# The start of the stationary weights in their ring buffers, one value for all segments against one for each

## The chip, the cores and the metric

The kernel runs on one core of a Trainium2 chip. The metric is the device time of one execution in microseconds. A core has engines that run side by side: TensorE (PE: matmuls, and PEld: the loads of their stationary operand), VectorE (DVE), ScalarE (ACT), GpSimd (POOL) and SyncE (SP), which here issues nearly all DMAs. TensorE reads both operands of a matmul from the on-chip memory SBUF: a 128x128 stationary part, which is loaded first, and then the moving columns, which stream past it into PSUM.

## The reference

One layer of a hybrid model over 256 tokens of width 1024: a modulated RMS norm of x, one projection `h @ w_in` to 11272 columns, a causal attention of eight heads with a relative bias (the query block has no earlier block here), a chunkwise mLSTM of four heads, two output projections, two sigmoid gates, and a last projection, added to x.

```
h = rmsnorm(x, norm_w) * (1 + scale) + shift          # shift, scale, gate from c @ w_ada + b_ada
qa, ka, va, za, qm, km, vm, zm, om, ig, fg, ga, gm = split(h @ w_in)
ya = (attention(rmsnorm(qa), rmsnorm(ka), va, rel_bias) * silu(za)) @ w_att_proj
qm, km = split(silu(causal_conv([qm, km])))
hm = rmsnorm(sigmoid(om) * mlstm(qm, km, vm, ig, fg))
ym = (hm * silu(zm)) @ w_ml_proj
out = x + gate * ((sigmoid(ga) * ya + sigmoid(gm) * ym) @ w_out)
```

## The kernel before

Each product of a projection is made of three passes in a reduced fp32 format (fp32r): an operand `a` is split into a high part (`a` rounded to fp32r) and a low part (`a` minus the high part), and the passes are high by high, high by low and low by high. A first phase makes `h`, transposed, as `hTh` and `hTl` (8 blocks of 128 features, 256 tokens each), and with it the columns of q and most of k. What follows is a list of 25 chunks of up to 512 columns, two to a segment (`va`, `za`, `qm`, and so on, in the order of the `seg` calls; the first chunk, of `ka`, stands alone). The loop that the program walks is over groups: one group is two of a chunk's eight blocks of 128 features, so there are four groups to a chunk.

Two kinds of chunk are told apart. In a `tok` chunk the stationary operand is a 128x128 part of `hTh` or `hTl` (`yh` or `yl` in the last segment) and the weights move, 512 columns at a time (lines 935 to 937, and 954 to 956 in the last chunk). In a `ws` chunk the weights are stationary: a group holds 24 matmuls (two feature blocks, four parts of 128 columns, three passes, lines 942, 944 and 945), and each loads a new 128x128 part of the weights and moves 256 columns of `hTh` or `hTl` past it. In `att` the moving tiles are `yah` and `yal`, in `ml` `ymh` and `yml`. The segments of the `ws` kind are `za`, `qm`, `km`, `att`, `ga`, `gm` and `ml`: 14 chunks, 1344 matmuls.

The weights of a group come by DMA into a tile `raw`, issued some groups ahead; `split` (line 416) then makes `wh` on ScalarE (line 423) and `wl` on VectorE (line 427; on GpSimd in eight groups) four groups ahead of the matmuls. `wh` and `wl` have five buffers each (`HB`), used in turn, so that group g uses buffer g mod 5. A buffer has 1152 floats to a partition (`RING`), 1024 of which are used: in a `tok` chunk from the buffer's start, in a `ws` chunk from float 80, which is byte 320 (`WS_AT`, line 25, used at lines 420 to 422).

Between groups the program puts other work of TensorE by hooks tied to the group's number: transposes against the identity (`ident`, lines 467, 604 to 606, 775), the attention's and the mLSTM's own products (lines 579, 617, 718, 738). The first matmul of a group after such work is called a restart here. The order of all work is written out by hand.

Of the kernel before, what the change touches and what calls it, by code (L numbers as in the profile page):

```python
# [21 lines left out]
NEG = -1e30  # L22
BUCKETS = 32

RING, WS_AT = 1152, 80

COL = dict(qa=0, ka=1024, va=2048, za=3072, qm=4096, km=5120, vm=6144, zm=7168, om=8192,
           ig=9216, fg=9220, ga=9224, gm=10248)
# [36 lines left out]
def tile_hybrid(ctx: ExitStack, tc: tile.TileContext, x, c, params, params2, rel_t, w_row, ada_mod, ada_gate,  # L65
# [232 lines left out]
    chunks = []  # L298
# [117 lines left out]
    def split(g, between=()):  # L416
        li, ks, cs = raw_of[g]
        w = rawt[li][:, ks, cs]
        n = chunks[g // 4]["n"]
        at0 = WS_AT if chunks[g // 4]["kind"] == "ws" else 0  # L420
        h = hl.tile([128, RING], F32R, name="wh", bufs=HB)[:, at0:at0 + 1024].rearrange("p (k n) -> p k n", k=2)[:, :, 0:n]
        l = hl.tile([128, RING], F32R, name="wl", bufs=HB)[:, at0:at0 + 1024].rearrange("p (k n) -> p k n", k=2)[:, :, 0:n]
        nc.scalar.copy(h, w)  # L423
        for fn, a in between:
            fn(*a)
        e = nc.gpsimd if g in pool_lo else nc.vector
        e.tensor_tensor(l, w, h.bitcast(F32), op=OP.subtract)  # L427
        whl[g] = (h, l)
# [462 lines left out]
    for g in range(A):  # L891
        split(g)
        for fn, a in early.get(g, []):
            fn(*a)
        consumed.update(li for li in cons.get(g, []) if li not in gate_loads)
    pump()
    for g in range(NG):
        ci, kp = divmod(g, 4)
        ch = chunks[ci]
        if g + A < NG:  # L900
            split(g + A, hooks_between.get(g, []))
            consumed.update(li for li in cons.get(g + A, []) if li not in gate_loads)
# [101 lines left out]
```

## Time and profile before

| | us |
|---|---|
| three timed executions | 355.11, 355.51, 355.52 |
| their median | 355.51 |
| the profiled execution | 354.88 |
| its span, first to last instruction | 353.1 |

The profiled execution's own time is 1.8 us more than its span. An engine's busy time is a sum over the span; matmuls are pipelined, so that the durations of two neighbours overlap. What a matmul costs in a stream is therefore not its duration but its pitch: the time from its start to the next one's start. The two go together for the `ws` matmuls, as the rows below show.

### The profile page before, as it was taken

What the parts mean: (1) busy time and instruction counts of PE and PEld (TensorE: products, weight loads), DVE (VectorE), ACT (ScalarE), POOL (GpSimd) and SP (SyncE); (2) the same over time, 40 slices, a digit from 0 to 9 for tenths busy, and PEclk for the clock granted to TensorE, in tenths of its full rate; (3) what the DMA queues carried; (4) which work ended last, traced back from release to release, by engine and by line L of the source; (5) the groups of instructions that cost most, each with busy time, mean ns of one, the idle gap of its engine ahead of it and who ended that gap; (6) DMA issues with size and microseconds to landing.
All of it is one profiled execution on the core that took longest, in us unless ns stands there. A gap on an engine that the chain in (4) does not pass through costs nothing.

```text
span 353.1 us, 5961 instructions
## 1 busy us (share of the span) xinstructions
PE 348.1 (99%) x2346; PEld 318.9 (90%) x2346; DVE 238.4 (68%) x362; ACT 212.7 (60%) x329; POOL 77.7 (22%) x89
## 2 busy tenths in 40 slices
PE   8999999999999999999999999999999999999995
PEld 5888889888999999999999888888899999999885
DVE  4799988879855528767774474764475775447773
ACT  3777799898786876674654435545646374534320
POOL 4920006583005043555240000000010320000000
PEclk9999999999999999999999999999999999999999
DMA  8999999994780463493664956749219129290011
GB/s 309 417 419 420 413 375 348 212 283 194 245 291 5 127 232 124 141 384 129 238 239 132 380 204 213 265 150 381 64 28 373 78 74 376 89 358 1 2 59 59
DMA packets 24573, 77.95 MB, mean 221 GB/s; under 512 B 2909, under 2 KB 5985, under 8 KB 24034
## 3 DMA queue, kind: packets, MB, share of 16 engines
q1 hardware_dynamic: 24240, 77.03, 61.2%
q10 hardware_dynamic: 306, 0.55, 0.5%
q8 instruction: 18, 0.29, 0.3%
q14 instruction: 9, 0.07, 0.1%
HBM read 76.12 MB, written 1.45 MB: 220 GB/s over the span
## 4 chain that ended last, share of the span: by engine, by line
PE 99%; DVE 0%; POOL 0%; issue 0%; POOLq 0%
PE mm L944 15%; PE mm L942 15%; PE mm L945 14%; PE mm L937 10%; PE mm L935 10%; PE mm L936 10%; PE pm L186 9%; PE pg L186 2%; PE xps L243 1%; PE pc L224 1%; PE mm L956 1%; PE mm L954 1%; PE aux L617 1%; PE warm L217 1%; PE mm L955 1%; PE aux L467 1%
## 5 line engine op out<-in xcount | busy, mean ns | idle before, releaser
L427 DVE TENSOR_TENSOR wl<-raw,wh 128x1024 fp32r<-128x1024 f32 (+1 forms) x92 | 112.5, 1234 | 66.9 <-ACT wh L423 66.9
L423 ACT CAST wh<-raw 128x1024 fp32r<-128x1024 f32 (+1 forms) x100 | 101.9, 1031 | 58.1 <-PE mm L937 29.7
L942 PE MATMUL mm<-hTh,wh 128*128 128x256 f32 x320 | 90.1, 282 | 0.0
L945 PE MATMUL mm<-hTh,wl 128*128 128x256 f32 x320 | 88.8, 278 | 0.0
L944 PE MATMUL mm<-hTl,wh 128*128 128x256 f32 x320 | 88.8, 278 | 0.0
L942 PEld LDWEIGHTS mm<-hTh,wh 128*128 128x128 f32 x320 | 60.4, 189 | 0.0
L944 PEld LDWEIGHTS mm<-hTl,wh 128*128 128x128 f32 x320 | 60.2, 188 | 0.0
L945 PEld LDWEIGHTS mm<-hTh,wl 128*128 128x128 f32 x320 | 60.1, 188 | 0.0
L935 PE MATMUL mm<-wh,hTh 128*128 128x512 f32 (+1 forms) x144 | 55.0, 382 | 0.0
L937 PE MATMUL mm<-wh,hTl 128*128 128x512 f32 (+1 forms) x144 | 54.4, 378 | 0.0
L936 PE MATMUL mm<-wl,hTh 128*128 128x512 f32 (+1 forms) x144 | 54.3, 377 | 0.0
L937 PEld LDWEIGHTS mm<-wh,hTl 128*128 128x128 f32 x144 | 27.0, 188 | 5.0
L936 PEld LDWEIGHTS mm<-wl,hTh 128*128 128x128 f32 x144 | 27.1, 188 | 4.7
L935 PEld LDWEIGHTS mm<-wh,hTh 128*128 128x128 f32 x144 | 27.0, 188 | 4.7
L427 POOL TENSOR_TENSOR wl<-raw,wh 128x1024 fp32r<-128x1024 f32 x8 | 19.6, 2463 | 17.9 <-ACT wh L423 12.6
L757 POOL TENSOR_SCALAR f<-f 128x4 f32<-128x4 f32 x2 | 0.4, 199 | 86.8 <-DVE f L756 86.8
L175 DVE TENSOR_TENSOR wrl<-raw,wrh 128x512 fp32r<-128x512 f32 (+1 forms) x24 | 18.0, 775 | 2.0 <-ACT wrh L170 1.7
L942 PE MATMUL mm<-yah,wh 128*128 128x256 f32 x64 | 18.0, 281 | 0.0
L944 PE MATMUL mm<-yal,wh 128*128 128x256 f32 x64 | 17.7, 277 | 0.0
L945 PE MATMUL mm<-yah,wl 128*128 128x256 f32 x64 | 17.7, 277 | 0.0
L942 PE MATMUL mm<-ymh,wh 128*128 128x256 f32 x64 | 17.7, 276 | 0.0
L944 PE MATMUL mm<-yml,wh 128*128 128x256 f32 x64 | 17.7, 276 | 0.0
(210 smaller groups left out, 648.9 us busy)
## 6 DMA issues: line engine op xcount, KB each, us to landing
raw<-in_w_in_dram SPq DMA_DIRECT2D x36, 1024.0 KB, 5.1
adat<-in_ada_mod_dram SPq DMA_DIRECT2D x16, 512.0 KB, 9.4
raw<-in_ada_gate_dram SPq DMA_DIRECT2D x4, 1024.0 KB, 5.7
raw<-in_w_att_proj_dram SPq DMA_DIRECT2D x4, 1024.0 KB, 7.5
raw<-in_w_ml_proj_dram SPq DMA_DIRECT2D x4, 1024.0 KB, 8.2
raw<-in_w_out_dram SPq DMA_DIRECT2D x4, 1024.0 KB, 5.6
raw<-in_w_row_dram SPq DMA_DIRECT2D x4, 896.0 KB, 12.3
raw<-in_w_row_dram SPq DMA_DIRECT2D x4, 640.0 KB
```

The costliest lines, as they stand in the source:

```text
L175: e.tensor_tensor(l[:, cs], wrow[k][:, cs], h[:, cs].bitcast(F32), op=OP.subtract)
L186: nc.tensor.matmul(pm[ch][:, t], a[:, k, t * 128:(t + 1) * 128], b[:, cs], start=k == 0 and i == 0 and (ch < 3 or t == 0), stop=k == KT - ...
L217: nc.tensor.matmul(pw[:, 0, 0:128], ident, ident, start=True, stop=True)
L224: nc.tensor.matmul(pc[n][:, 0:512], ones[0:1, :], crow[:, n * 512:(n + 1) * 512], start=True, stop=True)
L423: nc.scalar.copy(h, w)
L427: e.tensor_tensor(l, w, h.bitcast(F32), op=OP.subtract)
L935: nc.tensor.matmul(o, a, wh[:, kk], start=first, stop=False)
L936: nc.tensor.matmul(o, a, wl[:, kk], start=False, stop=False)
L937: nc.tensor.matmul(o, b, wh[:, kk], start=False, stop=last)
L942: nc.tensor.matmul(o, wh[:, kk, cs], sh_[:, k], start=first and i % 2 == 0, stop=False, skip_group_check=True)
L944: nc.tensor.matmul(o, wh[:, kk, cs], sl_[:, k], start=False, stop=False, skip_group_check=True)
L945: nc.tensor.matmul(o, wl[:, kk, cs], sh_[:, k], start=False, stop=last and i % 2 == 1, skip_group_check=True)
```

## The change

The one start of 80 floats for all `ws` chunks becomes a start by the segment's name: 84 floats (336 bytes) in `za` and `ml`, 80 (320) in `qm` and `km` as before, 76 (304) in `att`, 72 (288) in `ga` and 88 (352) in `gm`. The `tok` chunks have no entry and begin at the buffer's start, as before. The buffers keep their size and their places. No instruction is added, removed or moved on any engine and no wait differs: what differs is the address in the weight operand of 960 of the 1344 `ws` matmuls (five segments of 192), and in what the 80 instructions that fill those buffers write and, for `wl`, read.

```
-RING, WS_AT = 1152, 80
+RING = 1152
+WS_AT = dict(za=84, qm=80, km=80, att=76, ga=72, gm=88, ml=84)
...
         n = chunks[g // 4]["n"]
-        at0 = WS_AT if chunks[g // 4]["kind"] == "ws" else 0
+        at0 = WS_AT.get(chunks[g // 4]["name"], 0)
         h = hl.tile([128, RING], F32R, name="wh", bufs=HB)[:, at0:at0 + 1024].rearrange("p (k n) -> p k n", k=2)[:, :, 0:n]
         l = hl.tile([128, RING], F32R, name="wl", bufs=HB)[:, at0:at0 + 1024].rearrange("p (k n) -> p k n", k=2)[:, :, 0:n]
```

## Rows read from the trace of the kernel before

**Rows 1.** The page: busy time by engine, and the granted clock in 40 slices.

```profile
PE 348.1 (99%) x2346; PEld 318.9 (90%) x2346; DVE 238.4 (68%) x362; ACT 212.7 (60%) x329; POOL 77.7 (22%) x89
...
PEclk9999999999999999999999999999999999999999
```

**Rows 2.** Waits of PE over the span: line, releaser, total us, times, longest us.

```profile
PE warm L217 <- POOL ident masks.py:199: 1.4, 1, 1.4
```

**Rows 3.** The page: costliest groups, the splits of the weights and who they wait for.

```profile
L427 DVE TENSOR_TENSOR wl<-raw,wh 128x1024 fp32r<-128x1024 f32 (+1 forms) x92 | 112.5, 1234 | 66.9 <-ACT wh L423 66.9
L423 ACT CAST wh<-raw 128x1024 fp32r<-128x1024 f32 (+1 forms) x100 | 101.9, 1031 | 58.1 <-PE mm L937 29.7
```

**Rows 4.** Timeline of PE in `qm` and `km`: start us, duration us, line, operation.

```profile
130.01 0.28 PE L942 MATMUL mm<-hTh,wh 128*128 128x256 f32 x1
...
140.89 0.28 PE L942 MATMUL mm<-hTh,wh 128*128 128x256 f32 x1
```

**Rows 5.** Timeline of PE, fourth group of `za`: restart, and last three matmuls.

```profile
97.49 0.36 PE L942 MATMUL mm<-hTh,wh 128*128 128x256 f32 x1
97.69 0.28 PE L944 MATMUL mm<-hTl,wh 128*128 128x256 f32 x1
97.81 0.28 PE L945 MATMUL mm<-hTh,wl 128*128 128x256 f32 x1
...
100.28 0.28 PE L945 MATMUL mm<-hTh,wl 128*128 128x256 f32 x1
```

**Rows 6.** Groups by line, `za`'s first chunk: count, busy us, mean ns, idle before.

```profile
L945 PE MATMUL mm<-hTh,wl 128*128 128x256 f32 x32 | 9.0, 281 | 0.0
```

**Rows 7.** Groups by line, `za`'s second chunk.

```profile
L945 PE MATMUL mm<-hTh,wl 128*128 128x256 f32 x32 | 8.9, 278 | 0.0
```

**Rows 8.** Groups by line, `att`, both chunks.

```profile
L945 PE MATMUL mm<-yah,wl 128*128 128x256 f32 x64 | 17.7, 277 | 0.0
```

**Rows 9.** Groups by line, `ga`'s first chunk.

```profile
L945 PE MATMUL mm<-hTh,wl 128*128 128x256 f32 x32 | 8.9, 279 | 0.0
```

**Rows 10.** Groups by line, `ga`'s second chunk.

```profile
L945 PE MATMUL mm<-hTh,wl 128*128 128x256 f32 x32 | 9.0, 280 | 0.0
```

**Rows 11.** Groups by line, `gm`, both chunks.

```profile
L945 PE MATMUL mm<-hTh,wl 128*128 128x256 f32 x64 | 17.7, 276 | 0.0
```

**Rows 12.** Groups by line, `ml`, both chunks.

```profile
L945 PE MATMUL mm<-ymh,wl 128*128 128x256 f32 x64 | 17.7, 276 | 0.0
```

**Rows 13.** Timeline of PE, `tok` matmuls in the middle of the span.

```profile
192.19 0.39 PE L936 MATMUL mm<-wl,hTh 128*128 128x512 f32 x1
...
214.86 0.39 PE L937 MATMUL mm<-wh,hTl 128*128 128x512 f32 x1
```

**Rows 14.** Timeline of PE, the last segment: first 512-column matmul, first 256-column one.

```profile
327.17 0.39 PE L935 MATMUL mm<-wh,yh 128*128 128x512 f32 x1
...
343.86 0.28 PE L954 MATMUL mm<-wh,yh 128*128 128x256 f32 x1
```

**Rows 15.** Timeline of PE, last group of `ga`: restart, and last matmul.

```profile
280.37 0.37 PE L942 MATMUL mm<-hTh,wh 128*128 128x256 f32 x1
280.57 0.28 PE L944 MATMUL mm<-hTl,wh 128*128 128x256 f32 x1
280.69 0.28 PE L945 MATMUL mm<-hTh,wl 128*128 128x256 f32 x1
...
283.07 0.28 PE L945 MATMUL mm<-hTh,wl 128*128 128x256 f32 x1
```

**Rows 16.** Timeline of PE, `gm`'s first restart.

```profile
283.55 0.37 PE L942 MATMUL mm<-hTh,wh 128*128 128x256 f32 x1
283.75 0.28 PE L944 MATMUL mm<-hTl,wh 128*128 128x256 f32 x1
```

## The prediction

> **What bounds the kernel now.** I read the page first. PE is busy for 99% of the span at a granted clock of 9 tenths or more in every slice, its full 2.4 GHz level; DVE stands at 68%, ACT at 60% [rows 1]. The list of waits then says whether PE lacks anything: over the whole span it waits once, 1.4 us for the identity at the start [rows 2]. So the time is the sum of PE's pitches, and only what changes a pitch counts.
>
> The change touches two kinds of work. One is the filling of the ring buffers: a split costs 1.03 us on ACT and 1.23 us on DVE [rows 3], while a group of 24 matmuls takes at least 24 x 0.113 = 2.7 us, and four groups lie between a split and its use. What a shifted write costs is hidden by that. The cover would be gone if a split on either engine took over 2.7 us.
>
> The other is the `ws` matmuls. I read their starts in the timeline. Over one chunk in `qm` and `km`, 96 pitches lie between 130.01 and 140.89: 113.3 ns each [rows 4]. In the fourth group of `za` the 22 pitches from 97.69 to 100.28 are 117.7 ns each [rows 5]. Same instruction, same shapes, same clock: there is a fast and a slow gait, 4.33 ns apart. The duration shows the gait too: 276 ns goes with the fast and 281 with the slow, so a mean in the table by line tells how many of a stretch were slow. I read it at line 945 (line 944 agrees; line 942 holds the longer first matmul of each restart). `za`: 281 and 278 [rows 6, 7]; `att` 277 [rows 8]; `ga` 279 and 280 [rows 9, 10]; `gm` and `ml` 276, nothing slow [rows 11, 12].
>
> **The change part by part.** No instruction and no wait differs, so the sum has one term: slow pitches that go, less slow pitches that come.
>
> What there is to win, at 96 matmuls to a chunk and a slow share of (mean - 276) / 5: `za` 96 + 38, `att` 192 / 5 = 38, `ga` 58 + 77, together 307 slow matmuls x 4.33 ns = 1.33 us. The means are whole numbers; half a nanosecond off is 10 matmuls in a chunk, so the term is 1.1 to 1.5 us. I take 1.2, since the two means nearest to 276 rest on rounding most. `qm` and `km` keep their start and are no part of it.
>
> Not all of it can go. A restart begins slow wherever it is: in the last group of `ga`, which runs at 276 afterwards, the second pitch is still 0.12 us (280.57 to 280.69) [rows 15]. `za`, `att` and `ga` have 17 restarts by the timeline, the entry into `ga` counted; at one to five slow pitches, three in the middle, that is 17 x 3 x 4.33 ns = 0.2 us. So at best 1.2 - 0.2 = 1.0 us goes.
>
> What a pitch costs at a start that the trace does not show (304, 336, 288 and 352 bytes are in no row) I bound from both sides. Below: the 512-column matmuls, whose weights move and whose stationary part comes from another tile at another address, have 100 pitches from 192.19 to 214.86, 226.7 ns each [rows 13], which is twice 113.3. Two arrangements with the same time per column say that the fast gait is the moving stream's own, and no start brings it under 113.3. Above: in the last segment the 72 matmuls from 327.17 to 343.86 have 231.8 ns each [rows 14], 5.1 ns over 226.7; that is the dearest lasting gait near by, so 4.3 to 5.1 ns a slow matmul. If all 960 were slow at 5.1 ns it would be 4.9 - 1.2 = 3.7 us more than now, 359.2; if none were and the last segment, which follows `ml` with no restart, fell into step as well (72 x 5.1 ns = 0.37 us), 1.6 us less. I take the fast gait for most, because five of the seven segments show that a stretch holds it for long once it has it.
>
> A row bears on a rule here. Two gaits of one instruction at one clock mean that the load of the next stationary part and the moving stream do get into each other's way [rows 4, 5]. The Trainium skill, "SBUF — State Buffer", section "Who interferes with whom", gives TensorE two read ports of its own, one for the moving operand and one for the weight load, and calls them independent; by that rule no address could matter and the time would stay at 355.5. The rows speak against the rule as far as there are two gaits, and leave open whether the start address is what chooses between them.
>
> **The forecast.** The shifted starts keep the loads and the streams of `za`, `att` and `ga` from locking in the slow gait, `gm` and `ml` stay fast: 1.0 us less. The profiled execution goes from 354.88 to 353.9; the median of the runs shown is 355.51, 0.6 above the profiled one, and goes to 354.5.
>
> **The rivals.**
>
> *The gait is chosen by the restart and not by the address.* For it: the last group of the first `za` chunk and the last group of the second `ga` chunk are groups 15 and 75 of the walk, so both use buffer 0, and both meet the same blocks 6 and 7 of `hTh` and `hTl`. Every address is equal, yet the first is slow to its end and the second has (283.07 - 280.69) / 21 = 113.3 ns [rows 5, 15]. They differ in what stood before: attention transposes in one, transposes of `om` in the other, and in the first pitch, 0.20 us in both by two decimals. Against it: that shows that the address is not all, not that it is nothing; and four restarts of `za` in a row ended slow. The starts then only draw anew: some restarts that were slow become fast and the reverse. A group that changes gait is 24 x 4.33 ns = 0.10 us, and of some 20 restarts a few more may fall either way: 355.5, within 0.5 us.
>
> *The new starts put `gm` and `ml` into the slow gait.* This is the one on the slower side. Between the second matmul of `gm`'s first restart at 283.75 and the last segment at 327.17 there is no further restart: 383 matmuls at 113.4 ns [rows 14, 16]. All of them now stand at the floor, both segments get a new start, and nothing in between would break a slow gait once it is entered, as nothing breaks it in the 72 matmuls of the last segment. Price: 384 x 4.33 = 1.66 us, 2.0 at 5.1 ns. With `za`, `att` and `ga` unchanged the time is 355.5 + 1.7 = 357.2; with their gain as well 356.2. It decides from the point at which more slow matmuls come than go, about 1.0 / 0.00433 = 230 of the 384, when the gain comes true, and from 165 of them (0.71 us) when it does not. Against it: `qm`, `km`, `gm` and `ml` all hold the fast gait for dozens of matmuls with their present start, and a small step of 16 or 32 bytes need not change that.
>
> **How the numbers follow.** What a measurement of this kernel can tell from no change is 0.2%, 0.71 us. The forecast gets 0.50: the evidence that a slow gait exists is firm, the evidence that an address ends it is thin. Its own range is 353.9 (with the last segment in step) to 354.9; most of it, 0.43, lies under 354.8. The restart rival gets 0.32: 0.05 faster, 0.22 within, 0.05 slower. The slow `gm` and `ml` get 0.18: 0.15 slower, and 0.03 within, where the gain cancels it. That is 0.48 faster, 0.32 within (0.07 of it from the forecast) and 0.20 slower. The range from 353.8 to 356.7 holds the forecast, the restart rival and the slower case up to some way past its version with the gain; all 960 slow, at 359.2, lies outside, since even `za`, the slowest segment now, has a second chunk that is mostly fast [rows 7].
>
> **What would show each step.** PE without waits other than the first says that the sum of pitches still is the time. The mean at line 945 in each segment tells the gait: 276 or 277 in `za` and `ga` is the forecast, 278 to 281 spread over other chunks than now is the restart rival, 279 or more in `gm` or `ml` is the slower case. A pitch under 113 ns anywhere in a long stretch of the shifted segments would break the floor, a lasting one over 118.5 the upper bound, and a group in which PE waits for `wh` or `wl` the claim that the splits are covered. The `tok` chunks ought to keep 226.7 ns; if the last segment leaves its 231.8 ns, it is by what `ml` hands to it. The forecast is wrong if the time is not at least 0.7 us less, and its reason is wrong if the time falls and these means do not.

## The result, and the profile after

The changed kernel is slower: 358.94 us, the median of four executions (358.54 to 359.12), against 355.51 (355.11 to 356.25, four executions). The ratio is 1.0097, with a 95% interval of 1.0085 to 1.0109. The profiled execution took 358.91 us with a span of 357.1; that of before 354.88 with 353.1.

The page of the changed kernel, busy time and granted clock, and its list of PE's waits (line, releaser, total us, times, longest):

```profile
PE 352.2 (99%) x2346; PEld 323.4 (91%) x2346; DVE 237.9 (67%) x362; ACT 212.7 (60%) x329; POOL 79.0 (22%) x89
...
PEclk9999999999999999999999999999999999999999
```

```profile
PE warm L218 <- POOL ident masks.py:199: 1.4, 1, 1.4
```

The same picture as before [rows 1, 2]: the clock granted in full, one wait at the start, so the time is still the sum of PE's pitches. They have grown. The groups by line for the `wl` matmul (line 946 here, 945 before) over the whole of `za`, `att`, `gm` and `ml`, in this order, and last `qm`, which kept its start (count, busy us, mean ns):

```profile
L946 PE MATMUL mm<-hTh,wl 128*128 128x256 f32 x64 | 18.0, 282 | 0.0
...
L946 PE MATMUL mm<-yah,wl 128*128 128x256 f32 x64 | 18.0, 281 | 0.0
...
L946 PE MATMUL mm<-hTh,wl 128*128 128x256 f32 x64 | 18.0, 281 | 0.0
...
L946 PE MATMUL mm<-ymh,wl 128*128 128x256 f32 x64 | 17.9, 280 | 0.0
...
L946 PE MATMUL mm<-hTh,wl 128*128 128x256 f32 x65 | 18.0, 276 | 0.0
```

(`ga` prints the row of `gm`.) Every shifted segment stands at 280 to 282 ns, where before `za`, `att` and `ga` were a mixture and `gm` and `ml` stood at 276 [rows 6 to 12]; `qm` is at 276 as it was. The mean pitch in the shifted segments is now 118.7 ns in `za`, 117.8 in `att`, 118.3 in `ga`, 118.7 in `gm` and `ml`, and of their 926 pitches one is under 115 ns (113, the first one behind a restart in `ga`). The timeline from `gm`'s first restart to the last segment:

```profile
285.55 0.37 PE L943 MATMUL mm<-hTh,wh 128*128 128x256 f32 x1
285.76 0.28 PE L945 MATMUL mm<-hTl,wh 128*128 128x256 f32 x1
...
331.21 0.39 PE L936 MATMUL mm<-wh,yh 128*128 128x512 f32 x1
```

From the second matmul on that is 45.45 us for 383 matmuls, 118.7 ns each, where it was 113.4 [rows 14, 16]. That stretch alone, 45.66 us from the restart against 43.62, is 2.04 us longer.

| from the segment's first matmul to the next segment's, us | before | after | more |
|---|---|---|---|
| `za` | 30.42 | 30.86 | 0.44 |
| `qm`, `km` | 48.83 | 48.84 | 0.01 |
| `att` | 24.60 | 25.32 | 0.72 |
| `ga` | 26.17 | 26.54 | 0.37 |
| `gm`, `ml` | 43.62 | 45.66 | 2.04 |

The sum is 3.6 us. The spans differ by 4.0; the other 0.4 us lies in the first phase, ahead of the first matmul of `ka` (51.76 us before, 52.21 after), which the change does not touch and whose length differs by as much between the executions of other kernels below (51.8 to 53.0).

### The profile page after: what moved, and what is told of

The parts are those of the page before. It is cut to its first block, busy times and chain, and to the rows that moved or that the text cites. A ratio compares the mean times of both kernels' runs of the same rounds, so it can differ in the third digit from the quotient of the medians.

```text
span 357.1 us, 5961 instructions
## 1 busy us (share of the span) xinstructions
PE 352.2 (99%) x2346; PEld 323.4 (91%) x2346; DVE 237.9 (67%) x362; ACT 212.7 (60%) x329; POOL 79.0 (22%) x89
## 4 chain that ended last, share of the span: by engine, by line
PE 99%; DVE 0%; POOL 0%; issue 0%; POOLq 0%
PE mm L946 15%; PE mm L945 15%; PE mm L943 15%; PE mm L936 10%; PE mm L938 10%; PE mm L937 10%; PE pm L187 9%; PE pg L187 2%; PE xps L244 1%; PE mm L957 1%; PE pc L225 1%; PE mm L955 1%; PE mm L956 1%; PE aux L618 1%; PE warm L218 1%; PE aux L468 1%
## 5 line engine op out<-in xcount | busy, mean ns | idle before, releaser
L946 PE MATMUL mm<-ymh,wl 128*128 128x256 f32 x64 | 17.9, 280 | 0.0
```

The costliest lines, as they stand in the source:

```text
L946: nc.tensor.matmul(o, wl[:, kk, cs], sh_[:, k], start=False, stop=last and i % 2 == 1, skip_group_check=True)
```

## The experiments

In what follows *distance* is the start of the stationary part minus the start of the moving tile, modulo 256 bytes (steps between parts, blocks and buffers are multiples of 256 here). In the built program `hTh` and `hTl` begin 256 bytes past a multiple of 512, `yah`, `yal`, `ymh` and `yml` at one. A start of 80 floats is therefore distance 64 in all seven segments; the change made it 80 in `za` and `ml`, 48 in `att`, 32 in `ga` and 96 in `gm`. The pitches below are means over the timeline, first pitches of restarts (0.20 us) left out. e2 to e11 and e14 are one execution and one profile each, beside runs of the kernel before on the same chip.

**Two segments back (e1).**

```
-WS_AT = dict(za=84, qm=80, km=80, att=76, ga=72, gm=88, ml=84)
+WS_AT = dict(za=84, qm=80, km=80, att=76, ga=72, gm=80, ml=80)
```

> The changed kernel with gm and ml back at 80 floats (320 bytes), za, att and ga as changed. Theory A (a weight start that is no multiple of 64 bytes makes every 256-column matmul of its segment slow, about 118.7 ns a pitch for 113.3, and only that): gm and ml return to 113.3, 384 x 5.3 ns = 2.0 us less than the changed kernel, about 356.9; za, att, ga stay at 117.7 to 118.7. Theory B (the gait is drawn at a restart and then carried on; the new starts only drew badly): gm begins as it ended its restart in the changed kernel, slow for long, and the time stays within 0.5 us of 358.9, or gm and ml each fall either way.

Measured: 359.09 us, ratio to the kernel before 1.0117 (1.0085 to 1.0148). The gain of 2 us did not come. `gm` and `ml`, by line:

```profile
L946 PE MATMUL mm<-hTh,wl 128*128 128x256 f32 x64 | 18.0, 281 | 0.0
...
L946 PE MATMUL mm<-ymh,wl 128*128 128x256 f32 x64 | 18.0, 281 | 0.0
```

At the very start at which they ran at 276 before, they now run at 281, 117.8 ns a pitch for all of 381: theory B's picture. So a segment at distance 64 is not fast by itself; it can hold either gait for 45 us. Theory A as stated falls.

**One more segment back (e9), and the two segments alone (e10).**

```
+WS_AT = dict(za=84, qm=80, km=80, att=76, ga=80, gm=80, ml=80)     # e9
+WS_AT = dict(za=80, qm=80, km=80, att=80, ga=80, gm=88, ml=84)     # e10
```

> The changed kernel with ga, gm and ml back at 80 floats; za 84 and att 76 stay. Theory E (at 80 floats two gaits last, and a restart takes the one that the work before it leads to, so in the run before, gm and ml were slow at 80 because ga ahead of them was slow): ga shows its old mixture and gm and ml run at 113.3 again, 2.4 us less than the changed kernel, about 356.4. If it was something else than ga ahead of them, gm and ml stay at 117.8, about 358.2.

> The kernel before with the change in gm (88) and ml (84) alone, so that gm is entered from a ga as it was. Theory C (a distance other than 64 modulo 256 has no lasting fast gait): gm and ml at 118.7, 383 x 5.3 ns = 2.0 us over the kernel before, about 357.3. Theory B (only the entry decides, and it is the old one here): gm enters fast and stays at 113.3, 355.5.

Measured: e9 356.81, e10 357.72 (before 355.51). In e9 `ga` shows its old mixture group by group, and `gm` and `ml` are back at 113.4 and 113.3 ns. Their first restarts, e1 above and e9 below:

```profile
285.28 0.36 PE L943 MATMUL mm<-hTh,wh 128*128 128x256 f32 x1
285.48 0.28 PE L945 MATMUL mm<-hTl,wh 128*128 128x256 f32 x1
285.59 0.28 PE L946 MATMUL mm<-hTh,wl 128*128 128x256 f32 x1
...
330.58 0.39 PE L936 MATMUL mm<-wh,yh 128*128 128x512 f32 x1
```

```profile
285.51 0.37 PE L943 MATMUL mm<-hTh,wh 128*128 128x256 f32 x1
285.72 0.28 PE L945 MATMUL mm<-hTl,wh 128*128 128x256 f32 x1
285.83 0.28 PE L946 MATMUL mm<-hTh,wl 128*128 128x256 f32 x1
...
329.13 0.39 PE L936 MATMUL mm<-wh,yh 128*128 128x512 f32 x1
```

The two kernels differ in `ga`'s start alone. The same transposes stand before the restart, and its first two pitches come to 0.31 us in e1 and 0.32 in e9; with the one, `gm` and `ml` together take 45.30 us, with the other 43.62. What `ga` did ahead of it decides: theory E. To the nanosecond, which the timeline's two decimals hide, the first pitch is 202 in e1 and 207 in e9 and in the kernel before. That goes through all runs at distance 64 with the moving tiles at a multiple of 256 bytes: 41 restarts with a first pitch of 203 to 207 ns all ended fast, and of 71 with 200 to 202 ns 45 stayed slow.

e10 is the other half: `ga` and everything ahead of it are as before, and `gm` and `ml` have the changed starts:

```profile
L946 PE MATMUL mm<-hTh,wl 128*128 128x256 f32 x64 | 17.9, 280 | 0.0
...
L946 PE MATMUL mm<-ymh,wl 128*128 128x256 f32 x64 | 17.9, 280 | 0.0
```

117.3 and 118.7 ns, no pitch of 381 under 115, entered from the `ga` that leads to the fast gait at 80 floats. Theory B alone would have given 355.5. Both hold, then, at different starts: at distance 64 there are two lasting gaits and the restart takes one; at the changed distances only slow gaits were seen, and in `gm` (distance 96) also where it was entered as before.

**The moving tiles shifted (e2), and both shifted (e5).**

```
-    hTh = consts.tile([128, KT, S], F32R, name="hTh")               # hTl alike
+    hTh = consts.tile([128, 128 + KT * S], F32R, name="hTh")[:, 4:4 + KT * S].rearrange("p (k s) -> p k s", k=KT)
+WS_AT = dict(za=84, qm=84, km=80, att=80, ga=84, gm=80, ml=80)      # e2
+WS_AT = dict(za=84, qm=84, km=84, att=80, ga=84, gm=84, ml=80, ka=4, va=4, zm=4, vm=4, om=4)   # e5
-   ph.tile([128, NR], F32R, name="wrh", bufs=3)                     # e5; wrl alike
+   ph.tile([128, NR + 128], F32R, name="wrh", bufs=3)[:, 4:4 + NR]
```

> hTh and hTl, the moving tiles of five segments, begin 16 bytes further; weights at 84 floats (16 bytes past a multiple of 64, as the moving tiles then are) in za, qm and ga, at 80 in km, att, gm and ml. Theory A (the weights' own start counts): za, qm, ga slow at about 118.7 ns, km and gm fast at 113.3 but for restarts; the 512-column matmuls whose stationary part is hTh or hTl slow too, about 232 ns for 226.7. Theory C (the weights' start counts relative to the moving tile's, modulo 64): the reverse in the ws segments, za, qm, ga fast but for restarts, km and gm slow at about 118.7; the 512-column ones slow as well. att and ml, whose moving tiles stay, are as before in both.

> hTh, hTl and every tile that meets them on TensorE's other operand (wh and wl of za, qm, km, ga, gm, of the 512-column chunks, and of the first phase) begin 16 bytes further than in the kernel before; att, ml and the last segment as before. No operand of those segments begins at a multiple of 64 bytes any more, but the distance between the two operands is what it was. Theory C (the distance counts): as the kernel before, 355.5 within 1 us, qm and km at 113.3, 512-column matmuls at 226.9. Theory A (the weights' own start counts): 960 matmuls at 118 to 119 and the 512-column ones at 232, about 362.

Measured: e2 359.71 (before 355.45), e5 356.66 (before 355.14). In e2, `za`, `km`, `ga` and `gm` by line:

```profile
L946 PE MATMUL mm<-hTh,wl 128*128 128x256 f32 x64 | 17.7, 276 | 0.0
...
L946 PE MATMUL mm<-hTh,wl 128*128 128x256 f32 x65 | 18.4, 282 | 0.0
...
L946 PE MATMUL mm<-hTh,wl 128*128 128x256 f32 x64 | 18.1, 283 | 0.0
```

(`ga` prints the row of `za`.) The start of 84 floats that is slow throughout in the changed kernel is fast here, 113.7 to 114.3 ns in `za`, `qm` and `ga`, and 80 floats is slow, 119.2 in `km` and `gm`. Theory A is out and theory C holds: not the weights' place counts but their place against the moving tile's. It is not the place of the splits' writes either: in `za` they begin at 84 floats in both kernels. The 512-column matmuls of `zm`, `vm` and `om` went from 226.9 to 233.2 ns, as both theories had it. e5 says the same with all five segments at distance 64 and no operand at a multiple of 64 bytes: 113.4 to 114.2 ns. It also brought more than was expected. With both operands 16 bytes further every restart of `za` and `ga` ends fast after a few pitches, while in the kernel before 8 of the 14 stayed slow. And the 512-column matmuls, stationary part and moving weights both 16 bytes further, did not stay at 226.9: they have 231.1 ns, here 100 of them in `zm` and `vm`:

```profile
200.13 0.39 PE L937 MATMUL mm<-wl,hTh 128*128 128x512 f32 x1
...
223.24 0.39 PE L938 MATMUL mm<-wh,hTl 128*128 128x512 f32 x1
```

So the distance is not all; the same distance at another place behaves otherwise, better in one form and worse in the other. That, and a draw that went against `att` (0.6 us), is why e5 is 1.5 us over the kernel before and not at it.

**Other uniform starts (e3, e4, e6, e7) and small shifts (e8).**

```
+WS_AT = dict(za=96, qm=96, km=96, att=96, ga=96, gm=96, ml=96)      # e3; e4: all 64; e6: all 16; e7: all 112
+WS_AT = dict(za=81, qm=82, km=79, att=78, ga=79, gm=82, ml=81)      # e8
```

> All seven segments at 96 floats, 384 bytes, six times 64. Theory A: as the kernel before, fast in qm, km, gm, ml at 113.3 and a mixture after restarts in za and ga, 355.5 within 0.7 us. Theory D (320 bytes is good because it stands 64 bytes past the moving tiles' start modulo 128, and a start at the same place modulo 128 is bad): slow gaits of up to 120 ns everywhere, 1344 x 6.7 ns less the 1.3 us of now, about 363.

> All seven segments at 64 floats, 256 bytes, four times 64, which is also the moving tile's start modulo 512. Theory A: 355.5 within 0.7 us, fast in long stretches without restarts. Theory D: slow everywhere, about 363, and at this start at the latest, since the two streams then begin at the same place modulo 512.

> All segments at 16 floats, 64 bytes. The distance from the moving tile's start is then 320 modulo 512 in the hTh segments and 64 in att and ml: the two values of the kernel before, exchanged. Theory C with a period of 256 bytes: a fast gait of 113.3 is seen in long stretches in both kinds, the time 355 to 358 by which gait the restarts draw. If the period is 512 or the absolute place counts, the hTh segments are slow throughout, 118 or more, about 360.

> All segments at 112 floats, 448 bytes: a distance of 192 modulo 256 (64 before the moving tile's start instead of 64 after it). Theory C in its narrow form (only 64 after allows the fast gait): 117 to 120 ns everywhere, 360 to 363. Theory C with a mirror (a quarter of 256 away on either side): fast stretches at 113.3 as at 80 floats, 355 to 358.

> za and ml at 81 floats, qm and gm at 82, km and ga at 79, att at 78: distances of 68, 72, 60 and 56 modulo 256. Theory C, narrow: each is slow throughout, 117 to 119, about 361. If starts within the same 16 bytes are alike, 81 and 82 floats show fast stretches at 113.3 and 78 and 79 do not. If a shift of 4 to 8 bytes is too small to matter, all show the two gaits, 355 to 358.

Measured: e3 360.64 and e4 362.51 (before 355.45), e6 356.12, e7 360.31 and e8 360.86 (before 355.14). The pitches by distance, with all segments that had it (moving tile at a multiple of 64 bytes):

| distance | where | lasting pitch, ns |
|---|---|---|
| 64 | before, e6 | 113.3 or 117.7, by restart |
| 80 | `za`, `ml` changed | 118.7 |
| 96 | `gm` changed, e10 | 118.7, 117.3 |
| 128 | e3, all | 118.6 to 118.9 |
| 192 | e7, all | 117.8 (`ga` 117.3: one group fast) |
| 0 | e4, all | 119.7 to 120.0 |
| 32, 48 | `ga`, `att` changed | 118.3, 117.8 |
| 56, 60 | e8: `att`; `km`, `ga` | 117.9 (17 of 186 under 115); 119.5 |
| 68, 72 | e8: `za`, `ml`; `qm`, `gm` | 118.3; 118.3 |

Theory D's direction is right: a multiple of 64 is no help as such, and of all starts tried the same start modulo 256 is the slowest (120). The fast gait was seen beyond a single group at 64 alone, and 4 bytes off it is gone. Of the 84 restarts of e3, e4, e7 and e8 one ends fast, at 192, for the 22 pitches that its group has left; here their first and last matmul, then the rows by line of `gm` of e7 and of `km` of e8:

```profile
268.87 0.28 PE L945 MATMUL mm<-hTl,wh 128*128 128x256 f32 x1
...
271.36 0.28 PE L946 MATMUL mm<-hTh,wl 128*128 128x256 f32 x1
```

```profile
L946 PE MATMUL mm<-hTh,wl 128*128 128x256 f32 x64 | 17.9, 279 | 0.0
```

```profile
L946 PE MATMUL mm<-hTh,wl 128*128 128x256 f32 x65 | 18.3, 282 | 0.0
```

That these runs were slow ahead of most restarts is a rival, since at 64 a slow `ga` led to a slow `gm`. Against it: each of the four has restarts with a first pitch of 206 or 207 ns, which at 64 always ended fast, and they stayed slow. A fast segment ahead was tried only for 96 (e10) and for 48 with the moving tiles 16 bytes further (`km` and `gm` of e2).

e6 exchanges 320 and 64 modulo 512 between the segments and gives the gaits of the kernel before again, group by group: the same restarts stay slow (`za` 116.2, `att` 113.9, `ga` 116.3 ns, as before). That is the period of 256, and it says, as `za`, `att` and `ga` of e10 do, that the draws are no chance: the same sequence ahead of a restart leads to the same gait. (What e6 takes more than the kernel before lies ahead of the first matmul of `ka`, at 53.03 us for 51.76.) Four more rows by line, `za` and `gm` of e6, then `qm` of e4 and of e3:

```profile
L946 PE MATMUL mm<-hTh,wl 128*128 128x256 f32 x64 | 17.9, 280 | 0.0
...
L946 PE MATMUL mm<-hTh,wl 128*128 128x256 f32 x64 | 17.7, 276 | 0.0
```

```profile
L946 PE MATMUL mm<-hTh,wl 128*128 128x256 f32 x65 | 18.4, 283 | 0.0
```

```profile
L946 PE MATMUL mm<-hTh,wl 128*128 128x256 f32 x65 | 18.3, 281 | 0.0
```

**One pass of the three at another start (e14).**

```
+        al = 84 if chunks[g // 4]["kind"] == "ws" else 0
-        l = hl.tile([128, RING], F32R, name="wl", bufs=HB)[:, at0:at0 + 1024]...
+        l = hl.tile([128, RING], F32R, name="wl", bufs=HB)[:, al:al + 1024]...
```

> The kernel before with wl alone at 84 floats, wh at 80, in all ws segments. Of the three matmuls of a part, the one with wl is of line 946 here (945 before) and its weights are loaded while line 945 (944 before) moves hTl. Theory F (the load of the next part meets the columns that run meanwhile): the pitch from the hTl matmul to the wl matmul is the long one. Theory G (a part meets its own columns): the pitch from the wl matmul to the next is the long one. If one changed distance in three is enough to keep the whole sequence slow, no 113.3 is seen in long stretches, about 117 to 119 on the average and 359 to 361; if the other two bring it back each time, 114 to 115 and 356 to 357.

Measured: 360.32 (before 355.53). No lasting 113.3 anywhere; 117.8 ns in the long stretches. `gm` by line:

```profile
L946 PE MATMUL mm<-hTh,wl 128*128 128x256 f32 x63 | 17.7, 281 | 0.0
```

In the second chunk of `gm` the pitches after the `wh`, the `hTl` and the `wl` matmul are 115.8, 118.4 and 119.1 ns. One changed distance in three keeps the whole sequence slow, but two of the pitches are long, not one: neither F nor G is shown.

**Better starts for the 512-column chunks (e11).**

```
+WS_AT = dict(za=84, qm=84, km=84, att=80, ga=84, gm=84, ml=80, va=20, zm=36, vm=52, om=12)   # hTh, hTl as in e2
```

> hTh and hTl 16 bytes further with za, qm, km, ga, gm at 84 floats, and the moving weights of the 512-column chunks at other starts: va 20 floats, zm 36, vm 52, om 12 (80, 144, 208 and 48 bytes; distances of the stationary part from the moving one of 192, 128, 64 and 224 modulo 256). The ws segments as with both 16 bytes further: 113.4 to 114.3 with every restart ending fast. For the 512-column chunks no theory gives the place: where one of them is at 226.7, a kernel with the moving tiles 16 bytes further can beat the kernel before by the 0.8 us of za and ga; if all are at 230 or more, it can't in this way.

Measured: 356.97 (before 355.51). `va` 227.4 ns with some slow pitches after restarts, `vm` 226.7, `zm` 233.3, `om` 232.9. So the 512-column form has good places too with the moving tiles shifted: `va`'s weights at 80 bytes against `hTh` at 16 is the `ws` pair with the operands exchanged.

**Two attempts at the restarts (e12, e13).**

```
-        between(9 + h, att_qk, h)
         at(12 + h, att_PT, h)
+        at(9 + h, att_qk, h)                      # e12: all heads; e13: heads 3 to 6 only
         at(9 + h, att_exp, h)
...
-                T[nm] = t[:, at0:].rearrange("p (k s) -> p k s", k=KT)
+                T[nm] = t[:, 0:KT * S].rearrange("p (k s) -> p k s", k=KT)     # yh, yl
```

> The kernel before with two edits. In the attention the scores' matmuls of a head stand behind the transposes of an earlier one, not ahead of them, so that the restarts of za come after the scores; and yh and yl begin at the same place modulo 256 as the moving weights, not 64 and 192 bytes past it. Theory C and E: the last segment's 512-column matmuls fall from 231.8 to 227 as those of the other segments do at that distance, 0.3 us less; five restarts of za draw anew, 0.4 us less if they fall into the fast gait; together 354.8 to 355.2. If neither is so, 355.5.

> The kernel before with the scores of heads 3 to 6 alone behind the transposes (the restarts of groups 12 to 15), and yh and yl at the same place modulo 256 as the moving weights. Theory C and E: no new wait, three of those four restarts fall into the fast gait as in the run with all heads (0.3 us), the last segment's 512-column matmuls at 227 (0.3 us): 354.9, ratio 0.998 to 0.999. If the reorder costs a wait again or other restarts draw slow for it, 355.5 or more.

Measured: e12 358.49, ratio 1.0096 (1.0070 to 1.0123); e13 356.50, ratio 1.0024 (1.0011 to 1.0037). The gaits did what was expected: in both, four restarts of `za` that stayed slow before end fast and one that ended fast stays slow, so that `za` falls from 116.2 to 115.0 ns, and the last segment's 512-column matmuls fall from 231.8 to 227.0. PE's new waits in the attention, e12 and then e13, tell what ate it:

```profile
PE aux L618 <- DVE st L586: 2.4, 1, 2.4
```

```profile
PE aux L618 <- ACT PT L608: 0.9, 1, 0.9
```

Scores that start later leave the softmax behind a 1.2 us split on DVE, or its last step on ACT, when PE wants the probabilities: a gain of half a microsecond turned into a new wait of 2.4 and of 0.9. (In e12 PE also waited 0.6 us for a DMA of the first phase.) e12's expectation had no wait in it, and e13's "no new wait" was wrong. In e13 the wait and the gain account for the profiled execution (355.80 us) and not for the whole 1.0 us between the medians; the rest is open.

**The found starts for the whole kernel (e15).**

```
+WS_AT = dict(za=84, qm=84, km=84, att=84, ga=84, gm=84, ml=80, ka=20, va=20, zm=20, vm=20, om=20)
...      # hTh, hTl as in e2; wrh, wrl as in e5 but at 20; yah, yal begin at float 4; yh, yl as in e12
```

> hTh, hTl, yah, yal begin 16 bytes past a multiple of 256; the weights that meet them begin 80 bytes past one, stationary (za, qm, km, att, ga, gm at 84 floats) or moving (first phase, ka, va, zm, vm, om at 20 floats). ml as before, yh and yl at the same place as the moving weights. Order of all work as in the kernel before. By what the runs with the moving tiles 16 bytes further showed: za, qm, km, att, ga, gm at 113.4 to 114.4 with every restart ending fast (0.8 us less than the kernel before), va at 227.7, the other 512-column chunks at 226.7 to 227.5, the last segment at 227.2 (0.3 us less): 354.3, ratio 0.996 to 0.998. If the fast gait there was a matter of the draw, some of za, att and ga are slow again and the time is 355 to 356.

Measured: 354.55 us (354.31 to 355.25, 10 executions) against 355.49 (355.18 to 356.11, 14), ratio 0.9976 (0.9967 to 0.9986): faster than both kernels. `za` and `att` by line, then the timeline of the fourth group of `za` with its restart, and of the last segment:

```profile
L946 PE MATMUL mm<-hTh,wl 128*128 128x256 f32 x64 | 17.7, 276 | 0.0
...
L946 PE MATMUL mm<-yah,wl 128*128 128x256 f32 x64 | 17.6, 276 | 0.0
```

```profile
97.91 0.36 PE L943 MATMUL mm<-hTh,wh 128*128 128x256 f32 x1
98.11 0.28 PE L945 MATMUL mm<-hTl,wh 128*128 128x256 f32 x1
98.22 0.28 PE L946 MATMUL mm<-hTh,wl 128*128 128x256 f32 x1
...
98.69 0.28 PE L943 MATMUL mm<-hTh,wh 128*128 128x256 f32 x1
...
100.62 0.28 PE L946 MATMUL mm<-hTh,wl 128*128 128x256 f32 x1
...
326.93 0.40 PE L936 MATMUL mm<-wh,yh 128*128 128x512 f32 x1
...
343.28 0.28 PE L955 MATMUL mm<-wh,yh 128*128 128x256 f32 x1
```

(`ga` prints `za`'s row.) From 98.69 to 100.62 lie 17 pitches of 113.5 ns: the group that was slow to its end before [rows 5] is in step after six. What all pitches lie over 113.3 ns comes to 0.17 us in `za` (0.51 before), 0.07 in `att` (0.11) and 0.12 in `ga` (0.55), and the 72 matmuls of the last segment take 16.35 us against 16.69 [rows 14]: the expected gain by the means that were expected, and a time 0.25 us over the expected 354.3.

## Why the prediction was wrong

*The bound held.* PE waits once, the clock is full, and the growth of the shifted segments accounts for 3.6 of the 4.0 us of the spans. The cover of the splits held too: no wait for `wh` or `wl` appeared. So did the floor: no run has a lasting pitch under 113.3.

*The two gaits held* at the start of before, and so did the count of what there was to win: the pitches of `za`, `att` and `ga` lay 1.17 us over 113.3, where 1.2 was reckoned, and e15 takes 0.8 of it, where 1.0 was. At other starts there are more slow gaits than that one, from 117.3 to 120.0.

*The step that failed is the choice between the bounds:* "I take the fast gait for most, because five of the seven segments show that a stretch holds it for long once it has it." All those stretches were at one distance. They told how the gait behaves at 64 and nothing on 32, 48, 80 or 96, where no stretch was fast: 117.8 to 118.7 ns in all five segments, and e10 shows it for `gm` even behind the old `ga`. The price per slow matmul, bounded at 4.3 to 5.1 ns, measured 4.4 to 5.4. The upper bound, taken from the 512-column matmuls of the last segment, was broken in `za`, `gm` and `ml` (118.7, over the 118.5 that was named as the sign of it). That all 960 slow, reckoned at 359.2, comes so near to the 358.9 measured is in part luck: `att` cost less than the bound and those three more. I left that case out of the range with the argument that the second chunk of `za` is mostly fast, which is the same error: a row at the old start used for a new one. An unknown start deserved the whole bracket.

*The rival of the restarts* was half right: e1 and e9 show that what stood before a restart chooses the gait, at distance 64. Its own pair was weaker than it says: "every address is equal" holds for the operands, but chunks 3 and 18 write to different ones of the two `mm` buffers in PSUM; in e1 and e9 the output is the same too. It could not speak for other distances, and its 355.5 was wrong.

*The rival of slow `gm` and `ml`* named the largest part, 2.04 us against 1.66 to 2.0 reckoned, and its place. Its "against it", that a step of 16 or 32 bytes need not change the gait, is refuted by e10 for the 32 bytes of `gm`, and in e8 4 bytes do it. It came together with slow `za`, `att` and `ga`, 1.5 us more, which neither of its versions had.

*The rule weighed.* "SBUF — State Buffer" of the Trainium skill, section "Who interferes with whom", calls TensorE's two read ports independent. e2 against the changed kernel disagrees for fp32r operands as far as independent means that no address matters: the same weight start costs 113.7 to 114.3 ns or 118.7 by where the moving tile begins, and the distance alone moves the pitch between 113.3 and 120.0.

What stays open: by what mechanism the load and the stream hinder each other (e14 settles neither form); why a pair of starts 16 bytes further leaves the slow gait after every restart; and what in the work before a restart leads to the one gait or the other (the first pitch is a sign of it). That the distance acts through reads of the same part of SBUF is only a guess.

## What to carry to other kernels

Where TensorE is the bound and the trace shows two pitches for one form of matmul, look at where the stationary and the moving operand begin against each other before looking at the schedule, and change both ends. A pitch that holds for long at one setting need not hold at its neighbours; for a setting that no row shows, keep both bounds in the range. And an operand's start that is tuned in one segment can be undone by what the segment before it does, so it is judged over the whole span and not segment by segment.

## What was not expected of the hardware

In the runs above, at the full clock and with fp32r operands, a 128x128 stationary part and 256 moving columns take 113.3 ns in the fast gait and 117.3 to 120.0 out of it; 512 columns 226.7 against 231 to 233.3. The state is lasting: 383 matmuls in a row at one or the other, at the same addresses (e1, e9). It repeats with a period of 256 bytes (e6), is lost by 4 bytes (e8, one profile), and for the pair of starts 16 and 80 bytes past a multiple of 256 it is reached after every restart in `za`, `att` and `ga`, and holds for 512 columns with the operands exchanged (e15).
